# Keys before queries for B's first pair, and the residual's x loaded one slice per job

## The chip, the cores and the metric

The kernel runs on one core of a Trainium2 chip. The metric is the device time of one execution in microseconds (us). Times of engines and queues come from one profiled execution, counted from the start of its span.

## The reference

A decoder trunk of two layers over 1024 positions with 1024 channels. The change lies in layer 0, which reads (cut to what matters):

```
proj = (rmsnorm(x, g) * (1 + scale) + shift) @ w_in
a_q, a_k, a_v, b_q, b_k, b_v, f_logit, gate = split(proj)
a = swa_sink_attention(a_q, a_k, a_v, sinks, rel_bias)      # 8 heads, window 128, 2 key heads
b = forgetting_attention(b_q, b_k, b_v, log_sigmoid(f_logit + b_f))   # 8 heads, causal
x = x + gate_c * ((concat(a, b) * silu(gate)) @ w_out)      # the residual takes x once more
```

Layer 1 is a gated linear recurrence with a projection in, a convolution, a scan and a projection out; it is not touched.

## The kernel before, in words

All activations are kept with channels on the 128 partitions and positions along the free dimension, in two halves of 512 positions. A product of full precision is made of three matmuls: each operand is split into a high part (`hi`, a rounded copy made by ACT) and a low part (`lo`, the rest, made by POOL or DVE), and hi·hi, lo·hi and hi·lo are added up in PSUM.

**Attention.** The heads are worked in pairs: four pairs of A, then four of B. A pair is a row of units, each cut into steps: scores (S), a transpose of the probabilities on TensorE (T, `turn`), the product with the values (V, `product`) and, for A, an end step (E, `end`) that spreads the inverse sums with four transposes (`rbT_A`) and scales the output. A transposed block lies in one of the two PSUM buffers of the pool `psT` (`ps_t`); it is split by `split_t` (line 758) into `pth` (ACT) and `ptl` (DVE), and only then is its buffer free for the next transposes. The slots of lines 1052 to 1084 fix at which point each step comes.

**The fill.** Between these steps `weave` puts matmuls of projections that are needed later, so that TensorE always has something to do. `fill` (line 965) walks through a list of jobs. A job is a tile of weights, the k tiles, the activations and a `use` that takes the sums out of PSUM (tile `ps_fill`, two buffers); the weights of the next job are asked for when the job before it starts (line 980). While pair 3 of A is worked, the fill makes the queries and keys of B's first pair (`b_jobs(0)`, line 1018): `use_q` takes a half of the queries out of PSUM with two copies on ACT and two subtractions on DVE; `use_k` takes a half of the keys out with three copies on ACT, two subtractions and a copy on DVE, and two copies on POOL. The order of the two jobs is the list that `b_jobs` returns.

**The first out projection.** While the last pair of B is worked, the fill makes the first half of the out projection for seven of its eight k tiles: eight jobs, `o0_job(e)`, one for each tile of 128 output channels. At the end of each, `use_o0(e)` adds the sums to x on DVE (`residual`). That x is loaded again into the tile `x1_0`, whose memory is that of `hh_1` (the high part of the activations of the second half), which the fill of the pair before reads to its end. The eight loads, one per e, stand in a row at lines 1210 and 1211, just ahead of that `weave`.

**What sets the order.** TensorE's instructions stay in the order of the program (`ordered` holds "pe"). ACT, DVE, POOL and SP (the queue that issues nearly all DMAs) are put in order when the kernel is built, by a planner with an estimate of all durations: an instruction goes as soon as the planner has its inputs ready and its buffer free, the earlier one in the program first. `paced(name)` (line 87) pins instructions: each one issued inside it stays behind the instruction that the program has just before it on the same engine. On the chip each engine then takes its instructions strictly in that order, and one that waits holds up all behind it.

**Names.** `bq`, `khb`, `klb`: queries and high and low keys of B. `whi_o0a`, `wlo_o0a`: high and low weights of the eight jobs, split from `raw_o0a` as loaded. `pB`: a row of B's decay bias, loaded from DRAM (`gd`) on SP, masked at its end by POOL (`AFFINE_SELECT`), to which DVE adds the scores. Nearly all compute instructions are issued by one helper, so the profile gives L86 for them, and they are told apart by their tiles.

Of the kernel before, what the change touches and what calls it, by code (L numbers as in the profile page):

```python
# [27 lines left out]
KT = D // P  # L28
# [20 lines left out]
def hybrid_trunk(  # L49
# [43 lines left out]
    @contextmanager  # L93
    def paced(name):

        ordered.add(name)
        yield
        ordered.discard(name)

    act, dve, gp = Queue("act", nc.scalar), Queue("dve", nc.vector), Queue("gp", nc.gpsimd)  # L100
    pe, sync = Queue("pe", nc.tensor), Queue("sync", nc.sync)
# [38 lines left out]
    def hl_tile(slot, name, dt=F32R):  # L140
        return hl.tile([P, KT, HALF], dt, tag=f"hl{slot}", name=name)
# [56 lines left out]
    def t4(tag, name, dt=F32, bufs=None):  # L198
        bufs = bufs or BUFS[tag]
        return at.tile([P, 1024], dt, tag=tag, name=name, bufs=bufs)  # L200
# [97 lines left out]
    def split(raw, hi, lo, eng=gp):  # L298

        copy(hi, raw)  # L300
        sub(eng, lo, raw, r32(hi))
# [6 lines left out]
    def split_w(src, shape, name):  # L308
        return split_raw(load_w(src, shape, name), shape, name)
# [7 lines left out]
    def load_tile(src, name):  # L317
        parts = [split_w(src[:, 4 * i : 4 * i + 4], [P, 4, P], f"{name}_{i}") for i in range(2)]
        return [(parts[k // 4][0][:, k % 4], parts[k // 4][1][:, k % 4]) for k in range(KT)]
# [297 lines left out]
    def vtile(name):  # L617
        return at.tile([P, NB, 2, P], F32R, tag="V", name=name, bufs=2)

    va, vb0 = vtile("va"), vtile("vb0")  # L620
# [84 lines left out]
    def use_k(kh, kl):  # L705
        def use(h, ps):
            o = slice(h * HALF, (h + 1) * HALF)
            for hd, (a, b) in enumerate(((0, 64), (64, 0))):
                copy(kh[hd][a : a + 64, o], ps[a : a + 64])
                lo = kl[hd][a : a + 64, o]  # L710
                sub(dve, lo, ps[a : a + 64], r32(kh[hd][a : a + 64, o]))
                if hd:
                    dve.tensor_copy(kh[hd][b : b + 64, o], r32(kh[hd][a : a + 64, o]))
                else:
                    copy(kh[hd][b : b + 64, o], ps[a : a + 64])
                gp.tensor_copy(kl[hd][b : b + 64, o], r32(lo))

        return use
# [223 lines left out]
    def use_v(v, name):  # L942
        def use(h, ps):
            t = at.tile([P, HALF], F32, tag="tv", name=f"vt_{name}_{h}", bufs=1)
            copy(t, ps)

            def later():
                pt = ps_t(f"vT_{name}_{h}")
                for i in range(4):
                    tp(pt[:, i * P : (i + 1) * P], t[:, i * P : (i + 1) * P])  # L950
                for hd in range(2):
                    src = pt.rearrange("p (t h d) -> p t h d", t=4, h=2)[:, :, hd]
                    o = v[:, 4 * h : 4 * h + 4, hd]
                    copy(o[:, :, 0:64], src)
                    sub(dve, o[:, :, 64:128], src, r32(o[:, :, 0:64]))

            return later

        return use
# [36 lines left out]
    def lazy(make):  # L996

        got = []

        def get():  # L1000
            if not got:
                got.append(make())
            return got[0]

        return get

    def job(ti, name, use):
        return (lazy(lambda: load_tile(wt[ti], name)), range(KT), both, use)
# [4 lines left out]
    def q_job(ti, name):  # L1013
        q = lazy(lambda: qtiles(name))
        return q, job(ti, name, lambda h, ps: use_q(q(), name)(h, ps))

    def b_jobs(p):
        q, jq = q_job(T_BQ + p, f"bq_{p}")
        kh = lazy(lambda: [t4("KH", f"khb_{p}_{i}", F32R) for i in range(2)])
        kl = lazy(lambda: [t4("KL", f"klb_{p}_{i}", F32R) for i in range(2)])  # L1020
        jk = job(T_BK + p, f"bk_{p}", lambda h, ps: use_k(kh(), kl())(h, ps))
        if p == 0:
            return (lambda: (q(), kh(), kl(), vb0)), [jq, jk]
        v = lazy(lambda: vtile(f"vb{p}"))
        jv = job(T_BV + p - 1, f"bv_{p}", lambda h, ps: use_v(v(), f"bv_{p}")(h, ps))
        return (lambda: (q(), kh(), kl(), v())), [jq, jv, jk]
# [3 lines left out]
    for p in range(4):  # L1030
        q, jq = q_job(T_AQ + p, f"aq_{p}")
# [4 lines left out]
    for p in range(4):  # L1036
        src, js = b_jobs(p)
        jobs.append(js)
        starts.append(len(units))
        out = lazy(lambda p=p: heads_out(f"B_{p}"))  # L1040
        units += [unit_b(p, hd, j, src, out) for hd in range(2) for j in range(4)]
# [91 lines left out]
    def split_act(ti, h):  # L1133

        if h == len(yh):
            yh.append(hl_tile(3 * h, f"yh_{h}"))
            if h:
                tags = ("Q", "Q", "KH", "KL")
                yl.append(Parts([t4(t, f"yl_1_{i}", F32R) for i, t in enumerate(tags)]))
            else:  # L1140
                yl.append(hl_tile(1, "yl_0"))
        copy(yh[h][:, ti], gy[h][:, ti])
        sub(dve if ti % 2 and h else gp, yl[h][:, ti], gy[h][:, ti], r32(yh[h][:, ti]))
# [16 lines left out]
    def residual(xn, ps, lay, e):  # L1160
        dve.scalar_tensor_tensor(
            out=xn, in0=ps, scalar=mod[:, lay, 16 + e : 17 + e], in1=xn, op0=ALU.mult, op1=ALU.add
        )

    x1, w7, wo = [], [], []

    def use_o0(e):
        def use(h, ps):
            residual(x1[0][:, e], ps, 0, e)
            with paced("act"):  # L1170
                if e:
                    split_act(e - 1, 1)
            if e == 4:
                w7.append(at.tile([P, 2, KT, P], F32R, tag="V", name="w7"))
                for i in range(2):
                    es = slice(4 * i, 4 * i + 4)
                    raw = at.tile([P, 4, P], F32, tag="tv", name=f"w7raw_{i}", bufs=1)
                    sync.dma_start(raw, wo0.rearrange("e p k c -> p e k c")[:, es, KT - 1])
                    split(raw, w7[0][:, 0, es], w7[0][:, 1, es])

        return use

    def o0_job(e):
        def weights():
            with paced("act"):
                return load_tile(wo0[e], f"o0a_{e}")

        return (lazy(weights), range(KT - 1), lambda: {0: (yh[0], yl[0])}, use_o0(e))

    o0 = [o0_job(e) for e in range(KT)]  # L1190
    jobs.append(o0)
    jobs[7] = then_split(*jobs[7])
# [14 lines left out]


    x1.append(hl_tile(2, "x1_0", F32))
    for e in range(KT):  # L1210
        sync.dma_start(x1[0][:, e], xT[:, 0, e])
    split_act(KT - 2, 0)

    def load_o0c(e):
# [425 lines left out]
    for t0, tw in ((0, 512), (512, 256)):  # L1640
# [15 lines left out]
        for e in range(KT):  # L1656
            if t0 == 0 and e + 4 < KT:
                split_out(e + 4)
            w = wout[e]
# [161 lines left out]
```

## Time and profile before

| | |
|---|---|
| median of 3 runs | 871.53 us (871.23 to 871.74) |
| the profiled execution | 871.52 us, of it the span 869.7 us |
| mean granted TensorE clock | 0.996 |
| busy in the span: PE, DVE, ACT, POOL | 854.6, 573.7, 538.2, 374.6 us |
| DMA, mean over the span | 121 GB/s |

A row of a timeline gives start, duration, engine, operation, the tiles written and read, how many instructions were merged into the row, and in brackets how long the engine sat idle before it and what it waited for. `SPq` is the queue that issues DMAs; the time of its row is the issue, not the transfer. A row of the windows gives, for a stretch of time, the busy time of PE, PEld (weight loads), DVE, ACT and POOL with the number of instructions, the granted clock, the share of the DMA engines that were busy and the GB/s. In the list of waits stand the waiting tile, what ended the wait, the total in us, the count and the longest.

### The profile page before, as it was taken

Reading aid. Unit: us, or ns where it says so; the run is one execution under the profiler, and the core shown is the slowest. Engines: PE = TensorE matmul, PEld = TensorE weight load, DVE = VectorE, ACT = ScalarE, POOL = GpSimd, SP = SyncE. Lnnn points to the kernel's source line nnn. Section 1 sums busy time; section 2 is a strip of 40 time slices with the busy share of each in tenths; the row PEclk is TensorE's granted clock in tenths of the full one; section 3 lists DMA queues with packets and bytes.
Section 4 is the critical chain, followed back from the end, with each engine's and each line's share of the span. In section 5 each row is a group of like instructions: output and inputs, shape, how many; then the busy total and the mean of one; then the engine's idle time right before and its main releaser. Section 6 shows DMA issues by size and latency. Waiting matters only on the chain.

```text
span 869.7 us, 13308 instructions
## 1 busy us (share of the span) xinstructions
PE 854.6 (98%) x4553; PEld 724.7 (83%) x4553; DVE 573.7 (66%) x1131; ACT 538.2 (62%) x1052; POOL 374.6 (43%) x408
## 2 busy tenths in 40 slices
PE   9999999999999999999999999999999999999996
PEld 8788798888878888888888888878888877887996
DVE  7886567688777466566665678466676556973654
ACT  5766224688776565566766666457677666964731
POOL 4843232333342231232474554623655666875020
PEclk9999999999999999999999999999999999999999
DMA  9943772100113223223364464421212122226322
GB/s 342 403 180 128 222 238 76 43 25 25 37 44 115 89 80 125 93 90 119 100 209 143 158 206 170 134 78 61 80 55 73 44 66 80 96 86 205 111 109 86
DMA packets 54812, 104.88 MB, mean 121 GB/s; under 512 B 6888, under 2 KB 19632, under 8 KB 54232
## 3 DMA queue, kind: packets, MB, share of 16 engines
q1 hardware_dynamic: 53592, 102.98, 35.9%
q10 hardware_dynamic: 1152, 1.05, 0.4%
q8 instruction: 36, 0.59, 0.3%
q14 instruction: 32, 0.26, 0.1%
HBM read 95.07 MB, written 8.93 MB: 120 GB/s over the span
## 4 chain that ended last, share of the span: by engine, by line
PE 75%; DVE 6%; POOL 5%; DMA 5%; issue 4%; ACT 4%; SPq 0%; POOLq 0%; DVEq 0%; ACTq 0%
PE ps_fill L86 23%; PE ps_lx L86 6%; PE pst L86 6%; PE ps_o L86 5%; PE ps_o0c L86 5%; PE ps_lg L86 5%; PE oB L86 4%; PE ptB L86 3%; PE sB L86 3%; PE ps_t L86 3%; PE ps_v L86 3%; DMA ada<-in_ada_dram 2%; PE sA L86 2%; PE oA L86 2%; PE ptA L86 1%
## 5 line engine op out<-in xcount | busy, mean ns | idle before, releaser
L86 DVE TENSOR_TENSOR ptl_B<-ptB,pth_B 128x512 fp32r<-128x512 f32 (+1 forms) x80 | 50.9, 636 | 44.8 <-ACT pth_B L86 44.3
L86 ACT ACTIVATE pB<-pB,mnB 128x128 f32<-128x128 f32 (+3 forms) x64 | 49.5, 774 | 30.8 <-DVE mnB L86 30.5
L86 ACT ACTIVATE pth_B<-ptB 128x512 fp32r<-128x512 f32 (+1 forms) x80 | 44.1, 551 | 33.9 <-PE ptB L86 33.6
L86 DVE SCALAR_TENSOR_TENSOR xc_r<-ps_lx,col,xc_r 128x509 f32<-128x509 f32 (+2 forms) x48 | 35.6, 744 | 43.4 <-ACT xt_r L86 42.3
L86 POOL TENSOR_SCALAR_AFFINE_SELECT pB<-pB 128x128 f32<-128x128 f32 x64 | 19.0, 298 | 97.6 <-DMA pB<-gd 90.5
L86 PE MATMUL ps_o<-y1h,wo 128*128 128x512 f32 (+1 forms) x224 | 56.9, 342 | 0.7 <-POOL wo L86 0.7
L86 PE MATMUL pst<-hh,ws 128*128 128x512 f32 x192 | 55.4, 397 | 0.1
L86 PE MATMUL ps_lg<-h1h,wlo_lg 128*128 128x512 f32 x128 | 50.2, 392 | 0.9 <-POOL wlo_lg L86 0.7
L86 PE MATMUL ps_lx<-h1h,wlo_lx 128*128 128x512 f32 x128 | 50.4, 394 | 0.1
L86 PE MATMUL ps_lx<-h1l,whi_lx 128*128 128x512 f32 x128 | 50.3, 393 | 0.2 <-POOL h1l L86 0.2
L86 PE MATMUL ps_lx<-h1h,whi_lx 128*128 128x512 f32 x128 | 50.3, 393 | 0.0
L86 PE MATMUL ps_lg<-h1h,whi_lg 128*128 128x512 f32 x128 | 49.9, 389 | 0.0
L86 PE MATMUL ps_lg<-h1l,whi_lg 128*128 128x512 f32 x128 | 49.8, 389 | 0.0
L86 POOL TENSOR_TENSOR wlo_lx<-raw_lx,whi_lx 128x512 fp32r<-128x512 f32 x16 | 30.6, 1930 | 43.3 <-ACT whi_lx L86 34.0
L86 ACT ACT_TABLE_LOAD x35 | 44.9, 1283 | 5.1 <-issue 3.0
L86 PE MATMUL ptB<-ident,pB 128*128 128x128 f32 x288 | 45.0, 273 | 1.2 <-ACT pB L86 0.8
L86 PEld LDWEIGHTS ptB<-ident,pB 128*128 128x128 f32 x288 | 35.8, 140 | 11.7 <-ACT pB L86 1.7
L86 DVE CUSTOM_DVE_ANT_0 pB<-sB,pB 128x384 f32<-128x384 f32 (+2 forms) x64 | 35.2, 554 | 13.5 <-PE sB L86 7.7
L86 PEld LDWEIGHTS pst<-hh,ws 128*128 128x128 f32 x192 | 35.8, 188 | 9.3 <-issue 0.6
L86 PEld LDWEIGHTS ps_o<-y1h,wo 128*128 128x128 f32 x224 | 39.0, 189 | 5.5 <-POOL wo L86 1.1
L86 ACT ACTIVATE pA<-pA,mnA 128x256 f32<-128x256 f32 (+1 forms) x64 | 31.2, 488 | 11.5 <-DVE mnA L86 11.2
L86 PE MATMUL ps_o<-y1l,wo 128*128 128x512 f32 (+1 forms) x112 | 38.1, 340 | 0.0
(340 smaller groups left out, 2866.0 us busy)
## 6 DMA issues: line engine op xcount, KB each, us to landing
ada<-in_ada_dram SPq DMA_DIRECT2D x32, 512.0 KB
x<-in_xT_dram SPq DMA_DIRECT2D x20, 256.0 KB
ada<-in_ada_dram SPq DMA_DIRECT2D x4, 1024.0 KB
pB<-gd SPq DMA_DIRECT2D x8, 512.0 KB
raw_o0a<-in_wo_dram SPq DMA_DIRECT2D x16, 256.0 KB
raw_o0c<-in_wo_dram SPq DMA_DIRECT2D x16, 256.0 KB
x1d<-x SPq DMA_DIRECT2D x16, 256.0 KB
raw_lx<-in_wl_dram SPq DMA_DIRECT2D x16, 256.0 KB
```

Of the source, the lines that this page charges most:

```text
L86: ins = issue(*args, **kw)
```

## The change

Two edits. In `b_jobs` the two jobs of B's first pair trade places: keys first, then queries. And x for the residual of the first out projection is loaded in other places: slices 0 and 1 where all eight stood, and slice e + 1 right behind the loads of the weights of job e, for e from 1 to 6. (The weights of job 0 are asked for before `x1` holds a tile, so nothing is loaded with them.) The loads of the weights and of these slices are now also pinned on SP.

```diff
         if p == 0:
-            return (lambda: (q(), kh(), kl(), vb0)), [jq, jk]
+            return (lambda: (q(), kh(), kl(), vb0)), [jk, jq]
...
     def o0_job(e):
         def weights():
-            with paced("act"):
-                return load_tile(wo0[e], f"o0a_{e}")
+            with paced("act"), paced("sync"):
+                w = load_tile(wo0[e], f"o0a_{e}")
+                if e + 1 < KT and x1:
+                    load_x1(e + 1)
+                return w
...
+    def load_x1(e):
+        sync.dma_start(x1[0][:, e], xT[:, 0, e])
...
     x1.append(hl_tile(2, "x1_0", F32))
-    for e in range(KT):
-        sync.dma_start(x1[0][:, e], xT[:, 0, e])
+    for e in range(2):
+        load_x1(e)
     split_act(KT - 2, 0)
```

## The prediction

> **What bounds the kernel now.** I read the page first, then TensorE's waits, then the busy time by stretches of 10 us, and last the timelines around the two places that the change touches.
>
> ```profile
> span 869.7 us, 13308 instructions
> PE 854.6 (98%) x4553; PEld 724.7 (83%) x4553; DVE 573.7 (66%) x1131; ACT 538.2 (62%) x1052; POOL 374.6 (43%) x408
> ```
>
> TensorE is busy for 854.6 of 869.7 us. The change takes no matmul away and adds none, so all that it can give back is part of the 15.1 us in which TensorE stands. The list of its waits, largest first, shows what lies near the change.
>
> ```profile
> PE rbT_A L86 <- DVE ptl_A L86: 1.7, 1, 1.7
> ...
> PE oB L86 <- ACT pth_B L86: 0.5, 1, 0.5
> PE oB L86 <- DVE ptl_B L86: 0.4, 2, 0.2
> ```
>
> The longest single wait of TensorE in the whole kernel, 1.7 us, is that of the inverse sums of A (`rbT_A`) for DVE's `ptl_A`. The products of B (`oB`) wait for little. The stretches say where:
>
> ```profile
> 220.00:230.00 10.00, 10.00 (x60) 8.59 (x59) 7.74 (x20) 7.14 (x20) 0.79 (x4) 1.00 0.09 28
> 230.00:240.00 10.00, 10.00 (x63) 8.69 (x60) 6.33 (x19) 6.94 (x21) 5.28 (x9) 1.00 0.16 53
> ...
> 250.00:260.00 10.00, 8.23 (x58) 7.16 (x57) 8.69 (x26) 8.96 (x27) 4.48 (x11) 1.00 0.29 93
> ...
> 440.00:450.00 10.00, 9.57 (x64) 8.11 (x61) 5.76 (x15) 6.81 (x15) 8.06 (x10) 1.00 0.91 302
> 450.00:460.00 10.00, 10.00 (x59) 8.54 (x58) 6.27 (x16) 6.31 (x16) 5.10 (x7) 1.00 0.60 183
> 460.00:470.00 10.00, 9.63 (x51) 7.48 (x51) 5.27 (x14) 5.98 (x12) 5.55 (x6) 1.00 0.58 173
> ```
>
> In 250 to 260 TensorE is idle for 1.77 us, with ACT at 8.96 and DVE at 8.69 of 10: here A's last units meet the second half of B's keys, and ACT and DVE are the bound. In 440 to 450, where the eight loads of x stand, the DMA engines are at 0.91, but TensorE idles for 0.43 us only, then for 0.00 and 0.37. So the most that edit one can give is about 1.7 us and edit two about 0.8 us.
>
> **Edit one, keys ahead of queries.** The place in detail, TensorE, then ACT, then DVE:
>
> ```profile
> 253.41 0.60 PE L86 MATMUL ptA<-ident,pA 128*128 128x128 f32 x4
> ...
> 258.48 0.63 PE L86 MATMUL rbT_A<-ident,rb_A 128*128 128x128 f32 x4 [1.69 <-DVE ptl_A L86]
> ```
>
> ```profile
> 254.06 1.19 ACT L86 ACTIVATE khb<-ps_fill 64x512 fp32r<-64x512 f32 x2
> ...
> 256.80 0.60 ACT L86 ACTIVATE pth_A<-ptA 128x512 fp32r<-128x512 f32 x1
> ```
>
> ```profile
> 255.80 0.69 DVE L86 TENSOR_TENSOR klb<-ps_fill,khb 64x512 fp32r<-64x512 f32 x1
> 256.52 0.42 DVE L86 CAST khb<-khb 64x512 fp32r<-64x512 f32 x1
> ...
> 257.44 0.29 DVE L86 CUSTOM_DVE_ANT_0 pB<-sB,pB 128x128 f32<-128x128 f32 x1
> ...
> 257.65 0.69 DVE L86 TENSOR_TENSOR ptl_A<-ptA,pth_A 128x512 fp32r<-128x512 f32 x1
> ```
>
> `rbT_A` needs one of two transpose buffers. The one that comes free next holds the transposes of 253.41, done at 254.01; ACT takes them up only at 256.80, since it works through the key copies (254.06, two in a row, 1.19 us) and what has piled up behind. DVE has 0.69 and 0.42 us of the keys in its way too, and its `ptl_A` ends at 258.34. `rbT_A` starts 0.14 us later.
>
> What a half of queries and a half of keys cost:
>
> ```profile
> L86 ACT ACTIVATE bq<-ps_fill x4: 574/592/593, 225.9 to 236.8; 64x512 fp32r<-64x512 f32 x4
> L86 DVE SCALAR_TENSOR_TENSOR bq<-ps_fill,bq x4: 683/688/693, 226.5 to 237.4; 64x512 fp32r<-64x512 f32 x4
> ```
>
> ```profile
> L86 ACT ACTIVATE khb<-ps_fill x6: 576/592/596, 242.7 to 254.7; 64x512 fp32r<-64x512 f32 x6
> L86 DVE TENSOR_TENSOR klb<-ps_fill,khb x4: 676/689/695, 243.3 to 255.8; 64x512 fp32r<-64x512 f32 x4
> L86 DVE CAST khb<-khb x2: 422/422/423, 246.3 to 256.5; 64x512 fp32r<-64x512 f32 x2
> ```
>
> ```profile
> L86 POOL CAST klb<-klb x4: 605/698/866, 244.2 to 256.6; 64x512 fp32r<-64x512 f32 x4
> ```
>
> These views cover both halves. One half of queries: ACT 2 x 0.592 = 1.18 us, DVE 2 x 0.688 = 1.38 us, POOL nothing. One half of keys: ACT 3 x 0.592 = 1.78, DVE 2 x 0.689 + 0.422 = 1.80, POOL 2 x 0.698 = 1.40 us. With the order turned, the last half before B begins costs 0.59 us less on ACT and 0.42 us less on DVE. One of the two copies at 254.06 goes, so `pth_A` starts at about 256.21 and ends at 256.81; on DVE the copy at 256.52 goes, and `ptl_A` ends at 258.34 - 0.42 = 257.92 in the order of now, or at 256.81 + 0.69 = 257.50 if it is put ahead of the row of `pB`. The wait of 1.69 falls to between 1.27 and 0.85 us. I take 0.5 us of gain, near the order as it is. The bounds are 0 (the planner orders ACT or DVE another way and the time is not passed on) and the whole wait, 1.69. What is late next is the same chain for the following transposes: ACT stays nearly full up to 260.
>
> What moves the other way: keys now come out of PSUM at about 226 and 235 us, which puts 0.59 us on ACT, 0.42 on DVE and 1.40 on POOL twice. I cost it at nothing: TensorE shows 10.00 of 10 there, ACT has 2.9 and 3.1 us free in those stretches, DVE 2.3 and 3.7, POOL 9.2 and 4.7. With that cover gone it would be at most 2 x 0.59 = 1.2 us. The two pairs of weight loads that trade places are of one size, and DMA shares of 0.09 and 0.16 hide them. No wait is added: the first scores of B need the first half of both, and the later of the two comes out at about 243 us in either order.
>
> **Edit two, the loads of x.** SP's issues around the row, then POOL's steps on what was loaded, with an undisturbed load from another place for comparison:
>
> ```profile
> 435.64 2.38 SPq L86 DMA_DIRECT2D raw_o0a<-in_wo_dram  x2
> 439.82 3.65 SPq L86 DMA_DIRECT2D x<-in_xT_dram  x8
> 443.58 1.13 SPq L86 DMA_DIRECT2D pB<-gd  x2
> ```
>
>
> ```profile
> 449.25 0.29 POOL L86 TENSOR_SCALAR_AFFINE_SELECT pB<-pB 128x128 f32<-128x128 f32 x1 [1.77 <-DMA pB<-gd]
> ```
>
> ```profile
> 251.96 0.33 SPq L86 DMA_DIRECT2D pB<-gd  x1
> ```
>
> ```profile
> 254.90 0.29 POOL L86 TENSOR_SCALAR_AFFINE_SELECT pB<-pB 128x128 f32<-128x128 f32 x1 [0.49 <-DMA pB<-gd]
> ```
>
> The eight issues take 3.65 us, 0.46 each. Behind them, at 443.58, comes the bias for the next scores, and POOL gets it at 449.25, 5.67 us after its issue; the undisturbed load of 251.96 was there after 2.94 us. With six of the eight issues gone from the row, that bias is issued up to 6 x 0.46 = 2.7 us earlier and lands up to 2.7 us sooner after it. But TensorE's own waits here, 0.43 and 0.37 us, are not for this bias: the scores lie in PSUM meanwhile, and the fill goes on. So I take 0.2 us of the 0.8 us, with bounds of 0 and 0.8.
>
> The other side is that the loads of `raw_o0a` are now pinned. Six slices of x still have to go, each 0.46 us on SP, spread over the jobs. Their use is far off:
>
> ```profile
> L86 DVE SCALAR_TENSOR_TENSOR x<-ps_fill,mod,x x8: 743/748/751, 452.2 to 514.7; 128x512 f32<-128x512 f32 x8
> ```
>
> Eight residuals from 452.2 to 514.7 make (514.7 - 452.2) / 7 = 8.93 us for a job. Slice e + 1 is issued with the weights of job e, at the start of job e - 1, and used at the end of job e + 1: three jobs, 26.8 us, against a landing within 2.94 to 5.67 us. So these loads cost nothing; if SP held them by more than 21 us, the residual would wait. The Trainium skill speaks against this edit: "DMA: Bandwidth & Descriptors", Rules for kernel authors, says that a DMA should be issued early and waited for late, and the edit issues six loads later. By that rule the time would rise; it has its place among the rivals.
>
> The pin matters for the weights of job 1. In the kernel before, the two loads at 435.64 went ahead of the row of x (they are the second half of tile 1 and the first of tile 2, counted over the sixteen). Now both loads of tile 1 stand behind slice 1 in the program, and the slices wait for the memory of `hh_1`, to 439.82. So they are issued at 439.82 + 2 x 0.46 = 440.74 and at 441.20.
>
> ```profile
> L86 ACT ACTIVATE whi_o0a<-raw_o0a x16: 615/622/632, 432.0 to 498.9; 128x512 fp32r<-128x512 f32 x16
> ```
>
> ```profile
> 441.71 1.15 ACT L86 ACTIVATE whi_o0a<-raw_o0a 128x512 fp32r<-128x512 f32 x2
> 442.76 0.48 ACT L86 ACTIVATE pth_B<-ptB 128x384 fp32r<-128x384 f32 x1
> ```
>
> ACT's copies of tile 1 are the second pair of the sixteen, at 441.71. With a landing after 2.94 to 5.67 us the data are there at 443.7 to 446.9. Job 1 starts when job 0 ends, about 452.2, and needs 2 x 0.62 us on ACT and POOL's part between, so the weights themselves come in time. What is queued behind a copy that waits is all of ACT, first of all `pth_B`, for which TensorE's products wait. I expect the planner to move the copies behind the ACT work that is ready, which costs 0; the bounds are 0 and 5.2 us (446.9 - 441.71).
>
> **The sum.** The profiled execution took 871.52 us, 1.8 us more than its span, and the median of the runs, 871.53, is the same. 871.5 - 0.5 (keys) - 0.2 (row of x) = 870.8 us. A measurement of this kernel can tell about 0.2% from no change, 1.74 us; the forecast lies inside.
>
> **The rivals.**
>
> Rival one, the whole wait goes: the planner, with less in ACT's and DVE's way, puts `pth_A` and `ptl_A` ahead, and the waits of 440 to 470 shrink by half. For it speaks that the needed transposes were done at 254.01, so 4.3 us passed before they were out, of which only 1.3 us are work on them. Against it: ACT is at 8.96 of 10 and loses only 0.59. Time: 871.5 - 1.7 - 0.4 = 869.4 us.
>
> Rival two, slower: ACT waits at the copy of tile 1's weights. It decides if the planner's estimate of the landing is shorter than the chip's, so that the copy stays ahead of `pth_B`. For it speaks that POOL waited 1.77 us for a bias in the same crowd; against it that fewer loads now crowd there. ACT would stand from 441.71 to between 443.7 and 446.9, so 2.0 to 5.2 us; part of it falls into ACT's free time, and I take 2.5 us for TensorE: 871.5 - 0.5 + 2.5 = 873.5 us.
>
> Rival three, the load on ACT is only moved: the keys at 226 and 235 make a wait as large as the one that shrinks. Against it stands TensorE's 10.00 in both stretches. Time: 871.5 us.
>
> Rival four, by the rule above, the slices come late: a residual waits and keeps its PSUM buffer, so the fill stands. It needs a delay of over 21 us on SP. If it came, each of six jobs could lose up to a landing of 2.94 us; with one such loss 871.5 - 0.5 + 2.9 = 873.9 us.
>
> **How the numbers follow.** Forecast 0.46, rival one 0.30, rival two 0.13, rival three 0.08, rival four 0.03. Faster by over 0.2% (below 869.8) is rival one: 0.30. Slower by over 0.2% (above 873.3) is rivals two and four: 0.16. The rest, forecast and rival three, is 0.54. The range goes from 869.2, just below rival one, to 872.8, where the smallest of rival two's waits ends (871.5 - 0.5 - 0.2 + 2.0); left out are the lower part of rival one and the upper of rivals two and four, together about 0.2.
>
> **What would show it.** In the changed profile the keys leave PSUM near 226 and 235 us and the queries near 243 and 251; between 250 and 260 ACT falls by about 0.6 and DVE by about 0.4 us per the same work, and the wait of `rbT_A` stands at 0.8 to 1.3 us. SP shows two slices of x at about 440 and six single ones after it, and POOL's step on the next bias comes 3 to 5 us sooner than 449.25. Wrong would be a wait of `rbT_A` unchanged or gone, a new wait of TensorE at 220 to 240, or ACT's copies of `whi_o0a` waiting for a DMA with `pth_B` behind them and `oB` late at 444 to 448.

## The result, and the profile after

The changed kernel takes 874.94 us (median of 10 runs, 873.59 to 876.77) against 871.46 us for the kernel before in the same comparison. The ratio is 1.0033, with a 95% interval of 1.0024 to 1.0042: slower by about 3 us, on the other side of no change than the forecast of 870.8, and above the range's end of 872.8. Timed a second time on another chip (below) it gave 1.0029 (1.0018 to 1.0040). The profiled execution of after took 873.92 us with a span of 872.1; before it was 871.52 and 869.7. So the two traces, laid side by side, have to account for 2.40 us. That is near the difference of the medians on the second chip (874.36 - 871.92 = 2.44), and 1.1 us less than the one on the first, where the profiled execution of after was its second fastest of ten. Two executions far out of line, one of 2359.56 us in the second timing of the change and one of 1717.87 us with `w7raw` apart in the kernel before, are counted in the medians and left out of the ratios.

The list of TensorE's waits of the changed kernel, largest first and cut to two lines (total, count, longest in us):

```profile
PE ptB L86 <- ACT pB L86: 3.2, 3, 2.4
...
PE rbT_A L86 <- DVE ptl_A L86: 0.9, 1, 0.9
```

One wait has shrunk, `rbT_A` from 1.7 to 0.9 us. Another stands at the head of the list now: the transposes of B's probabilities wait for ACT 3.2 us in all, where it was 0.8 in the kernel before, and 2.4 us of that is a single new wait. The stretches of the changed kernel that answer to those of before:

```profile
220.00:230.00 10.00, 10.00 (x60) 8.59 (x59) 7.16 (x20) 7.60 (x21) 1.98 (x6) 1.00 0.08 28
230.00:240.00 10.00, 10.00 (x62) 8.69 (x61) 6.95 (x21) 7.52 (x22) 6.33 (x12) 1.00 0.15 53
250.00:260.00 10.00, 8.93 (x64) 7.86 (x63) 8.61 (x25) 8.78 (x27) 2.96 (x9) 1.00 0.33 91
440.00:450.00 10.00, 7.60 (x40) 6.36 (x39) 3.97 (x12) 6.17 (x14) 7.02 (x9) 0.83 0.63 204
```

Between 250 and 260 TensorE is idle for 1.07 us in place of 1.77 and does 64 matmuls in place of 58; at 220 to 240, where the keys now leave PSUM, it is still at 10.00. That is edit one, and it works. Between 440 and 450 TensorE does 40 matmuls where before it did 64, and the granted clock is 0.83, which is 3.4 us at half clock.

Where the time went can be read off by counting matmuls: their order on TensorE is fixed but for the two jobs that trade places, so the start of the n-th one can be compared between two traces. Difference to the kernel before, in us, from the starts in each trace:

| n-th matmul (start in before) | 1400 (253.05) | 1500 (271.04) | 2480 (441.03) | 2500 (444.78) | 2550 (453.17) | 2700 (480.21) | last (862.48) |
|---|---|---|---|---|---|---|---|
| after | -0.05 | -0.80 | -0.86 | +1.43 | +2.20 | +2.34 | +2.35 |

The keys win 0.8 us near 255 us, and this is kept for 170 us. Then 2.29 us are lost within 20 matmuls, 0.77 more within the next fifty, and 0.15 after that: -0.81 + 2.29 + 0.77 + 0.15 = 2.40 us from the 1400th matmul on, or 2.35 with the 0.05 that after was ahead there. After the 2700th nothing more is lost.

The place of the loss in the changed kernel. First SP's issues:

```profile
438.96 0.81 SPq L86 DMA_DIRECT2D x<-in_xT_dram  x2
439.82 0.90 SPq L86 DMA_DIRECT2D raw_o0a<-in_wo_dram  x2
440.76 0.43 SPq L86 DMA_DIRECT2D x<-in_xT_dram  x1
441.30 0.84 SPq L86 DMA_DIRECT2D pB<-gd  x2
```

Next ACT, with the time that it stood idle in brackets:

```profile
440.84 0.49 ACT L86 ACTIVATE pth_B<-ptB 128x384 fp32r<-128x384 f32 x1
444.12 0.63 ACT L86 ACTIVATE whi_o0a<-raw_o0a 128x512 fp32r<-128x512 f32 x1 [2.79 <-DMA raw_o0a<-in_wo_dram]
444.66 1.13 ACT L86 ACTIVATE pB<-pB,mnB 128x1024 f32<-128x1024 f32 x1
...
445.79 0.61 ACT L86 ACTIVATE whi_o0a<-raw_o0a 128x512 fp32r<-128x512 f32 x1
```

And TensorE:

```profile
443.26 0.27 PE L86 MATMUL ptB<-ident,pB 128*128 128x128 f32 x1
445.93 0.55 PE L86 MATMUL ptB<-ident,pB 128*128 128x128 f32 x3 [2.40 <-ACT pB L86]
```

Read backwards: TensorE's three transposes wait for the exponentials of a row of 1024 of `pB`. ACT makes these at 444.66, right after its copy of tile 1's weights, and that copy had stood at the head of ACT's queue since 441.33 for a load that SP issued at 439.82. In the kernel before, the same row of 1024 was made at 443.13, with no wait ahead of it:

```profile
443.13 1.15 ACT L86 ACTIVATE pB<-pB,mnB 128x1024 f32<-128x1024 f32 x1
```

A copy whose result was wanted about ten microseconds later (job 0's last step, the residual, is at 454.41) held up work that TensorE needed at once.

### The profile page after: what moved, and what is told of

It is laid out like the page before. It is cut to its first block, busy times and chain, and to the rows that moved or that the text cites. A ratio compares the mean times of both kernels' runs of the same rounds, so it can differ in the third digit from the quotient of the medians.

```text
span 872.1 us, 13306 instructions
## 1 busy us (share of the span) xinstructions
PE 855.7 (98%) x4553; PEld 725.7 (83%) x4553; DVE 573.5 (66%) x1131; ACT 538.2 (62%) x1052; POOL 374.1 (43%) x408
## 3 DMA queue, kind: packets, MB, share of 16 engines
q10 hardware_dynamic: 1152, 1.05, 0.4%
## 4 chain that ended last, share of the span: by engine, by line
PE 76%; DVE 6%; DMA 6%; POOL 4%; ACT 4%; issue 3%; SPq 1%; POOLq 0%; DVEq 0%; ACTq 0%
PE ps_fill L86 23%; PE ps_lx L86 6%; PE ps_lg L86 6%; PE pst L86 6%; PE ps_o L86 5%; PE ps_o0c L86 5%; PE oB L86 4%; PE sB L86 3%; PE ptB L86 3%; PE ps_v L86 3%; PE ps_t L86 3%; DMA ada<-in_ada_dram 2%; PE sA L86 2%; PE oA L86 1%; PE ptA L86 1%
```

## The experiments

The theory: the loss comes from the pin of the weights' loads on SP, which puts tile 1's loads behind the slices of x; ACT then stands at its copy. The rivals: keys first costs something later; the slices of x as such cost; the fall of the granted clock after the wait is a loss of its own. The kernels of each table row ran on one chip with the kernel before between them.

| run | median, us | before, us | ratio (95%) |
|---|---|---|---|
| keys first alone | 871.24 | 872.20 | 0.9987 (0.9978 to 0.9996) |
| x per job with pins alone | 875.17 | 872.20 | 1.0036 (1.0024 to 1.0049) |
| pin of the weights alone | 874.64 | 872.20 | 1.0032 (1.0019 to 1.0044) |
| change, weights not pinned | 871.82 | 872.20 | 1.0000 (0.9992 to 1.0009) |
| change, weights ahead of x | 871.16 | 871.56 | 0.9996 (0.9988 to 1.0005) |
| change, TensorE busy in the wait | 874.05 | 871.56 | 1.0027 (1.0016 to 1.0037) |
| weights not pinned, w7raw apart | 869.95 | 871.56 | 0.9982 (0.9973 to 0.9991) |
| the change again | 874.36 | 871.92 | 1.0029 (1.0018 to 1.0040) |
| TensorE busy in the wait, again | 874.10 | 871.92 | 1.0023 (1.0012 to 1.0033) |
| before, w7raw apart | 871.31 | 871.92 | 0.9997 (0.9988 to 1.0006) |
| keys first, w7raw apart | 871.08 | 871.92 | 0.9988 (0.9980 to 0.9997) |

The profiled executions of these runs, by the same count of matmuls against the kernel before:

| n-th matmul | 1400 | 1500 | 2480 | 2500 | 2550 | 2700 | last |
|---|---|---|---|---|---|---|---|
| keys first alone | +1.05 | +0.29 | +0.26 | +0.25 | +2.58 | +2.38 | +2.49 |
| x per job with pins alone | +0.51 | +0.52 | +0.52 | +2.85 | +3.00 | +3.68 | +3.62 |
| pin of the weights alone | +0.81 | +2.32 | +2.32 | +1.99 | +4.24 | +4.23 | +4.17 |
| weights not pinned | -0.01 | -0.82 | -0.87 | -0.87 | -1.08 | -0.17 | -0.22 |
| weights ahead of x | +0.03 | -0.72 | -0.79 | -0.79 | -1.06 | -0.40 | -0.46 |
| not pinned, w7raw apart | +0.08 | -0.71 | -0.73 | -0.73 | -1.00 | -2.30 | -1.65 |
| the change again | +0.33 | -0.42 | -0.42 | +1.50 | +2.60 | +2.86 | +2.83 |
| before, w7raw apart | +0.13 | +0.07 | -0.03 | -0.04 | +0.20 | -1.11 | -0.95 |
| keys first, w7raw apart | +0.66 | -0.10 | -0.03 | -0.04 | +0.70 | -0.57 | -0.34 |

What a row has at the 1400th matmul is from ahead of both edits; only what it gains or loses from there on counts.

**Keys first alone.**

```diff
-            return (lambda: (q(), kh(), kl(), vb0)), [jq, jk]
+            return (lambda: (q(), kh(), kl(), vb0)), [jk, jq]
```

> The kernel before with the keys ahead of the queries and nothing else. Theory (the loss is all in the loads, the keys gain): the wait of the inverse sums of A falls from 1.69 to about 0.95 us as in the changed kernel, no wait of 2.4 us at 443, granted clock 1.00 in 440 to 450; time 0.7 us under the kernel before, about 870.8. Rival (the keys spoil the plan of ACT later on): slower than the kernel before by over 1 us.

Faster, 871.24 against 872.20 us, and its wait of `rbT_A` is 0.9 us. Edit one is a small gain by itself. The execution that was profiled was this kernel's slowest (874.08) and shows something else. POOL stood for the next bias, and ACT then for DVE's row maximum over it. POOL, then ACT:

```profile
451.53 0.54 POOL L86 TENSOR_SCALAR_AFFINE_SELECT pB<-pB 128x128 f32<-128x128 f32 x2 [4.30 <-DMA pB<-gd]
```

```profile
452.19 0.40 ACT L86 ACTIVATE pB<-pB,mnB 128x128 f32<-128x128 f32 x1 [4.06 <-DVE mnB L86]
```

That bias was issued at 443.84, behind the row of eight slices, and POOL got it 7.7 us later, where it was 5.67 us in the kernel before. In this execution 2.33 us are lost between the 2500th and the 2550th matmul; TensorE waits 1.32 us there for `pth_B`, and the granted clock is at half from 454.6 to 458.0. So the row of eight does cost something, in some executions; it is the thing that edit two was to take away.

**x per job with its pins alone, queries first as before.**

```diff
-            with paced("act"):
-                return load_tile(wo0[e], f"o0a_{e}")
+            with paced("act"), paced("sync"):
+                w = load_tile(wo0[e], f"o0a_{e}")
+                if e + 1 < KT and x1:
+                    load_x1(e + 1)
+                return w
...
-    for e in range(KT):
+    for e in range(2):
```

> The loads of x one slice per job and pinned with the weights, queries ahead of keys as before. Theory: the long wait of the transposes near 444 us (2.4 us in the changed kernel) and the dip of the granted clock stay, the wait of the inverse sums stays at 1.69; time about 0.7 us over the changed kernel and 4 us over the kernel before, about 875.5. Rival (the keys made it): no such wait, 871.5.

The whole loss is here. ACT of this run, then TensorE:

```profile
445.54 0.63 ACT L86 ACTIVATE whi_o0a<-raw_o0a 128x512 fp32r<-128x512 f32 x1 [2.83 <-DMA raw_o0a<-in_wo_dram]
```

```profile
447.36 0.55 PE L86 MATMUL ptB<-ident,pB 128*128 128x128 f32 x3 [2.45 <-ACT pB L86]
```

The waits are those of after, 2.79 and 2.40 us there, although the queries come first: keys first has no part in the loss.

**The pin of the weights alone; x stays in one row of eight.**

```diff
-            with paced("act"):
+            with paced("act"), paced("sync"):
                 return load_tile(wo0[e], f"o0a_{e}")
```

> The kernel before with its eight slices in one row, queries first, and only the loads of the eight weight tiles pinned on SP. Theory (the pin makes it): the loads of tile 1 stand behind all eight slices, are issued near 443.5 and land near 449; ACT stands at the copy or, with the copy planned later, the weights come closer to their use at 452; a wait of TensorE of 1 to 4 us, time 872.5 to 876. Rival (the spreading of the slices makes it): as the kernel before, 871.5.

No slice of x is moved here, and the time, 874.64 us, is near that of the run above, with overlapping intervals. SP, then ACT:

```profile
442.15 3.65 SPq L86 DMA_DIRECT2D x<-in_xT_dram  x8
445.85 0.98 SPq L86 DMA_DIRECT2D raw_o0a<-in_wo_dram  x2
```

```profile
452.25 0.63 ACT L86 ACTIVATE whi_o0a<-raw_o0a 128x512 fp32r<-128x512 f32 x1 [3.04 <-DMA raw_o0a<-in_wo_dram]
```

With the pin, tile 1's loads stand behind all eight slices, and ACT waits 3.04 us. The copy stands elsewhere in ACT's order than in the change, behind the row of 1024, and TensorE's longest wait here is one of 1.02 us for `pth_B`. The execution that was profiled is this kernel's slowest (875.67). Of what it is behind, 1.5 us were lost between the 1400th and the 1500th matmul, where the clock was at half and which lies long before tile 1's loads; 1.9 us were lost from the 2480th on. So one word of code, in a line that the change gives no weight to, is enough for a loss of about that size, by a wait of the same kind.

**The change with the slices pinned and the weights not.**

```diff
-            with paced("act"), paced("sync"):
+            with paced("act"):
                 w = load_tile(wo0[e], f"o0a_{e}")
+            with paced("sync"):
                 if e + 1 < KT and x1:
                     load_x1(e + 1)
-                return w
+            return w
```

> The changed kernel with the pin on SP taken from the weights and left on the slices of x, so keys first and one slice per job, but the weights of tile 1 free to be loaded ahead of the slices. Theory: tile 1 is loaded near 401 and 435 us as in the kernel before, ACT doesn't stand at its copy, no clock dip; time about 870.7. Rival (one slice per job costs by itself): 873 to 875 as the changed kernel.

The wait of 2.4 us is gone, and the time is 871.82 us, where I had expected about 870.7. By the matmuls, the keys' gain is kept to the 2500th (-0.87) and 0.21 us more is won by the 2550th. But it ends level with the kernel before. ACT, then TensorE:

```profile
461.42 0.63 ACT L86 ACTIVATE w<-w7raw 128x512 fp32r<-128x512 f32 x1 [3.58 <-DMA w7raw<-in_wo_dram]
462.07 0.60 ACT L86 ACTIVATE pth_B<-ptB 128x512 fp32r<-128x512 f32 x1
```

```profile
462.72 0.51 PE L86 MATMUL oB<-pth_B,vb 128*128 128x256 f32 x2 [0.72 <-ACT pth_B L86]
```

It is the same pattern at a second place: a copy of weights (the eighth k tile, `w7raw`, whose second load has to wait until the first is split, since they share a buffer) stands ahead of `pth_B` on ACT. The copy can start at about the same time as in the kernel before, so whoever comes earlier only waits longer:

```profile
461.63 0.63 ACT L86 ACTIVATE w<-w7raw 128x512 fp32r<-128x512 f32 x1 [2.69 <-DMA w7raw<-in_wo_dram]
```

One comparison on this chip is against the slices: keys first with x in one row took 871.24 us, 0.58 less than this run. The loss at `w7raw` may be the reason, but keys first alone was profiled only in its slowest execution, so it isn't shown that it does not lose as much there.

**The change with tile 1's weights asked for ahead of the slices.**

```diff
+    o0[1][0]()
     x1.append(hl_tile(2, "x1_0", F32))
-    for e in range(2):
+    for e in range(3):
         load_x1(e)
```

> The change with everything pinned as it is, but the two loads of tile 1's weights issued ahead of the two x slices of the row, so ahead of the wait for the memory of hh_1 that held them to 439.82 us. If the loss comes from the copies of tile 1's weights standing on ACT for a late load (2.79 us of wait at 444.12, 2.40 us of TensorE's), SP should show those loads before 437 us, ACT's copies should stand without a wait near 442, TensorE's wait of ptB for pB should be under 0.3 us, and the time should be that of the change less 2.3 to 3.1 us: 870.8 to 871.8 us. If pinning on SP as such costs (the queue held in the order of the program), or the later issue of the x slices does, the time stays over 873 us although the wait of ptB is gone.

SP of this run (the first row has some idle time of the queue between its two issues, the second is at 434.63):

```profile
429.90 5.06 SPq L86 DMA_DIRECT2D raw_o0a<-in_wo_dram  x2
439.03 1.29 SPq L86 DMA_DIRECT2D x<-in_xT_dram  x3
```

```profile
440.40 1.15 ACT L86 ACTIVATE whi_o0a<-raw_o0a 128x512 fp32r<-128x512 f32 x2
```

Everything is pinned here as in the change, the slices go one per job after the first three, as there, and the loss is gone: 871.16 us. So neither the pin nor the slices cost the 2 to 3 us as such. What costs is the place of two loads: in the change they are issued at 439.82, 1.5 us before ACT is ready for them (441.33), and here by 434.63, 5.8 us ahead of the copy.

**TensorE kept busy in the wait.** The single transpose at 443.26 is made 25 times over, on the same data.

```diff
-                    tp(pt[:, w : w + P], prs[r][:, m * P : (m + 1) * P])
+                    for _ in range(25 if (hx, j, m, r) == (5, 3, 0, 0) else 1):
+                        tp(pt[:, w : w + P], prs[r][:, m * P : (m + 1) * P])
```

> The change with the one 128x128 transpose that stood alone before TensorE's wait of 2.40 us (ptB at 443.26) done 25 times over instead of once, so TensorE is at work in what was a wait; it rewrites the same block, the result is the same, and ACT waits for its load as before. In the change the granted clock fell to half for 3.4 us right after that wait. If the half clock follows from TensorE's idling, it should not be seen near 446 to 450 us in this run, the clock's mean should be higher by about 0.004, and the time should be 0.7 to 1.5 us under the change's: 873.4 to 874.2 us, still over the kernel before. If the half clock comes from something else, or the wait of ACT alone is the whole loss, the time stays within 0.4 us of the change's 874.9.

> The changed kernel once more, unaltered, on the same chip as the next run, because the two were so far timed on different chips and their ratios to the kernel before (1.0033 and 1.0027) lie within each other's intervals. Expected as before: 874 to 876 us. If the profiled execution shows no interval of half clock after the wait of 2.4 us, that interval is not a fixed consequence of the wait.

> The run with the transpose repeated 25 times in the wait, unaltered, beside the change on one chip. Its profiled execution had no half clock near 446 us and a wait of ACT of 3.04 us, and ended as late as the change's. If the half clock is a regular part of the change's loss, this stays 0.5 to 1.0 us under the change on the same chip. If it is only there in some executions and ACT's wait is the loss, the two agree within 0.4 us.

The first run with the wait filled took 874.05 us, inside the 873.4 to 874.2 that I had written for a half clock that costs. But it ran on another chip than the change, and its ratio of 1.0027 lies inside the change's interval; so the two were timed again side by side.

The reason for this pair of kernels is a row of the stretches of after, right behind the wait (the clock is the last number but two):

```profile
446.50:449.50 3.00, 3.00 (x13) 2.57 (x13) 2.41 (x7) 2.05 (x6) 2.37 (x4) 0.50 0.13 37
```

TensorE's clock was granted at half for some 3 us. The change again, on another chip: its wait, and the stretch behind it:

```profile
446.00 0.55 PE L86 MATMUL ptB<-ident,pB 128*128 128x128 f32 x3 [2.03 <-ACT pB L86]
```

```profile
446.50:449.50 3.00, 2.67 (x14) 2.09 (x13) 2.34 (x7) 2.00 (x6) 1.43 (x4) 0.60 0.39 113
```

And the second run with the wait filled, TensorE and the same stretch:

```profile
443.32 3.22 PE L86 MATMUL ptB<-ident,pB 128*128 128x128 f32 x28
```

```profile
446.50:449.50 3.00, 2.31 (x16) 1.85 (x15) 2.15 (x7) 2.14 (x7) 2.39 (x4) 1.00 0.71 217
```

This fits a half clock that comes from TensorE's standing: 0.50 and 0.60 with the wait, 1.00 in both filled runs, while ACT waited as long in them (2.73 us in this one). Two executions of each are few, as the next case shows. But on one chip the two kernels take 874.36 and 874.10 us, 0.26 apart, inside the 0.4 that I had put down for "ACT's wait is the loss". The profiled pair tells why: the filled kernel gains 0.63 us on the change by the 2520th matmul, and by the 2650th all but 0.15 of it is given back, since the steps behind wait for ACT and DVE. The waits of the filled kernel's TensorE between 440 and 470 us:

```profile
PE ptB L86 <- DVE ptl_B L86: 0.7, 1, 0.7
PE oB L86 <- ACT pth_B L86: 0.6, 1, 0.6
```

In the change on the same chip these two are 0.3 us and none. The run of x per job with pins says the same of the loss. It had a wait of 2.45 us and no half clock behind it:

```profile
447.50:450.50 3.00, 2.27 (x16) 1.84 (x16) 2.00 (x7) 1.99 (x6) 2.78 (x6) 1.00 0.25 75
```

and it still lost 3.62 - 0.52 = 3.1 us behind the 2480th matmul, as after did (2.35 + 0.86 = 3.2). So the half clock is there in the records, but as a term of the loss it can't be told from nothing here.

**w7raw's two loads in two jobs.** First in the kernel with unpinned weights, then in the kernel before, then with keys first and x in one row:

```diff
-            if e == 4:
+            if e == 3:
                 w7.append(at.tile([P, 2, KT, P], F32R, tag="V", name="w7"))
-                for i in range(2):
+            if e in (3, 4):
+                i = e - 3
...
-                    split(raw, w7[0][:, 0, es], w7[0][:, 1, es])
+                with paced("act"):
+                    split(raw, w7[0][:, 0, es], w7[0][:, 1, es])
```

> The run with the pin on the x slices alone (no pin on the weights' loads), and besides it the two loads and splits of the eighth k tile's weights (w7raw, one buffer for both) asked for in two jobs, e = 3 and e = 4, in place of both in e = 4. There ACT waited 3.58 us at 461.42 for the second w7raw load (2.69 in the kernel before), and about 0.9 us of the keys' gain was lost in the same stretch. If that wait gave the gain away, it should be under 1 us here, and the time 870.5 to 871.1 us, under the kernel before by about 0.9 us. If the gain is lost to something else (ACT's copies themselves, or the x slices' place), the time stays within 0.3 us of that run's 871.8.

> The kernel before, and only w7raw's two loads and splits in jobs e = 3 and e = 4 with the copies pinned on ACT, in place of both in e = 4. No edit of the change in it. ACT's wait of 2.69 us for the second load should go. If the gain of that edit stands by itself, 870.3 to 871.2 us against about 871.6; if it only gives back what the x slices' move had cost, within 0.3 us of the kernel before.

> Keys ahead of queries, the eight x slices in one row as before, and w7raw's two loads and splits in two jobs. Against the run that has both of these and x one slice per job (869.95 us, ratio 0.9982) it tells what the x slices' move itself is worth with no load of weights held up by it: if the row of eight costs by holding the next bias, this is 0.3 to 0.8 us slower than that run (870.3 to 870.8); if the move is worth nothing, the same (869.7 to 870.2).

ACT's copies in the first of the three:

```profile
478.94 0.62 ACT L86 ACTIVATE w<-w7raw 128x512 fp32r<-128x512 f32 x1
488.57 0.63 ACT L86 ACTIVATE w<-w7raw 128x512 fp32r<-128x512 f32 x1 [0.67 <-DMA w7raw<-in_wo_dram]
```

The wait of 3.58 us is 0.67 now. Between the 2550th and the 2700th matmul, where the kernel without this edit lost 0.91 us (-1.08 to -0.17), this one wins 1.30 more (-1.00 to -2.30), and it keeps half of that to the end. The time is 869.95 us, the fastest version of this study at 0.9982 of the kernel before (0.9973 to 0.9991), whose interval leaves out both no change and the kernel after. I had expected 870.5 to 871.1 us, about 0.9 under the kernel before; it is 1.6 us under (871.56 - 869.95). In the kernel before the same edit took 0.6 us off the median, but its interval of 0.9988 to 1.0006 holds no change. ACT's wait for the second load is gone there, and the time lies between my two cases. With keys first and the row of eight the ratio is 0.9988, and 871.08 us is outside both ranges that I had given. The profiled execution of that one loses 0.74 us between the 2500th and 2550th matmul, where the one with x per job gains 0.27. ACT of the two, in that order:

```profile
450.81 0.40 ACT L86 ACTIVATE pB<-pB,mnB 128x128 f32<-128x128 f32 x1 [2.97 <-DVE mnB L86]
```

```profile
447.19 0.40 ACT L86 ACTIVATE pB<-pB,mnB 128x128 f32<-128x128 f32 x1
448.25 0.51 ACT L86 ACTIVATE pB<-pB,mnB 128x256 f32<-128x256 f32 x1 [0.56 <-DVE mnB L86]
```

The same step on a row of 128 stands 2.97 us behind the row of eight and not at all behind three slices. By the trace that is worth 1.0 us. By the times 0.9982 and 0.9988 on two chips, whose intervals overlap, it isn't shown.

## Why the prediction was wrong

**What bounds the kernel: right.** TensorE's waits were all there was to win or lose; the 2.40 us between the two profiled executions are found in them and in what follows on them.

**Edit one: right in mechanism, low in size.** I took 0.5 us with a remaining wait of 0.85 to 1.27. It is 0.95:

```profile
256.15 0.60 ACT L86 ACTIVATE pth_A<-ptA 128x512 fp32r<-128x512 f32 x1
...
256.86 0.69 DVE L86 TENSOR_TENSOR ptl_A<-ptA,pth_A 128x512 fp32r<-128x512 f32 x1
...
257.69 0.63 PE L86 MATMUL rbT_A<-ident,rb_A 128*128 128x128 f32 x4 [0.95 <-DVE ptl_A L86]
```

`pth_A` starts at 256.15 (256.21 was worked out) and `ptl_A` ends at 257.55 (257.50, for the case that DVE puts it ahead of the row of `pB`). Of the two cases that I gave, the better one came; TensorE gained 0.75 us by the 1500th matmul. The cover for the keys at 225 to 240 held, with TensorE at 10.00.

**Edit two, the row of x: right on the bias, not shown as a gain.** POOL's step on the next bias came at 446.05 in place of 449.25, 3.2 us sooner, within the 3 to 5 that I named (0.9 of it is the lead that the keys had won):

```profile
446.05 0.29 POOL L86 TENSOR_SCALAR_AFFINE_SELECT pB<-pB 128x128 f32<-128x128 f32 x1
```

In the change that is not seen in the time, because the new wait lies on top of it. Without that wait the 0.2 us that I took is there in the traces: 0.21, 0.27 and 0.27 us are won between the 2500th and 2550th matmul in the three runs that keep the slices apart and do not hold up the weights. Three runs with the row of eight and no pin lose 0.24, 0.74 and 2.33 us there, all against the one execution of the kernel before, which has the row too. In the times it isn't shown: on one chip the row of eight was 0.58 us the faster (871.24 against 871.82), and with `w7raw` apart the slices were ahead, but on two chips and with overlapping intervals. The six slices later on cost nothing, as said: the eight residuals of after, at 454.4 to 517.1, waited for TensorE's sums or for nothing, never for x:

```profile
462.56 0.75 DVE L86 SCALAR_TENSOR_TENSOR x<-ps_fill,mod,x 128x512 f32<-128x512 f32 x1 [1.60 <-PE ps_fill L86]
...
509.36 0.75 DVE L86 SCALAR_TENSOR_TENSOR x<-ps_fill,mod,x 128x512 f32<-128x512 f32 x1 [0.22 <-PE ps_fill L86]
```

So rival four did not come true for x. What was issued late, at a cost, were the loads beside x, the weights.

**The pin of the weights: the step that failed.** Its first half stood. Both loads behind the slices, at 440.74 and 441.20: they went at 439.82 and 440.34. Landing at 443.7 to 446.9: ACT's copy began at 444.12. Then came "I expect the planner to move the copies behind the ACT work that is ready, which costs 0; the bounds are 0 and 5.2 us". It moved one of the two, to 445.79. The other stayed where it was, and the term was 2.29 us on TensorE, plus 0.77 and 0.15 behind it, in which lie the half clock and the steps that followed late; their shares aren't shown. Up to this place the keys alone had won 0.8 us, as much as both terms of gain in the sum (0.7), so this term put the time on the other side of no change.

It was not the only term that was missing. With the pin off the weights the ratio was 1.0000 (0.9992 to 1.0009), with the forecast's 0.9992 at the very end of the interval. The trace has 0.91 us lost between the 2550th and the 2700th matmul, where ACT waits for `w7raw`. The sum had no term for that place.

Rival two was this case. Its place and price were nearly those measured (873.5 us; 2.5 us on TensorE), and it got 0.13. It had one detail wrong: `pth_B` was not behind the copy but ahead of it, at 440.84; what stood behind was the exponentials. Was there a reason in what I had before me for another weight? One: the code pins the copies on ACT as well, so a copy can move back only as far as the program's order and the planner's own estimate of the load let it, and my step gave it a freedom that nothing in the trace of before showed. There the two copies at 441.71 had no wait at all and so told nothing about what the planner does with late data. That the planner thought the data would be there by 441 is my reading of the order; no run shows its estimate.

The range ended at 872.8, below rival two's full price; with that rival at 0.13 and rival four above it, the upper end cut off the case at its full price, which is what came.

## What to carry to other kernels

A load is in time if it lands before its consumer comes up in its engine's order; that can be long before the result is needed. When a change puts loads in a new order on the issuing queue, look for the consumer's place in its engine's order, and ask what stands behind it. A pin that is added along with an edit is an edit of its own and wants a price of its own; here it cost more than the two edits gave. And where a gain melts away later, look for a second place of the same kind: the late `w7raw` took back 0.7 to 0.9 us in two runs, and nothing in the one with its loads put apart.

## What the runs showed of the hardware

A wait of TensorE of some 2 us can be followed by half clock: behind 2.40 and 2.03 us in the change, and in the run with the pin alone behind the same wait of 1.7 us for `ptl_A` that the kernel before has:

```profile
261.00:264.00 3.00, 3.00 (x13) 2.73 (x12) 1.84 (x7) 1.10 (x4) 1.98 (x3) 0.50 0.00 0
```

In the slowest execution of keys first alone it stood behind a wait of 1.32 us. It does not always follow: not behind 2.45 us in the run of x per job with pins, nor behind the 1.69 us in the profiled execution of the kernel before. That may be part of why single executions of one kernel lie 2 to 3 us apart (870.8 to 873.87 for the kernel before); it wasn't tested. The Trainium skill, "TensorE: Matmul & The Clock Gate", Why this matters for your kernels, asks that no gap exceed about 3 us. Here waits of 1.3 to 2.4 us stood ahead of half clock in some executions, so what was measured is stricter. The Trainium skill, the same page, Part 1, says that the window in which activity is judged runs freely and does not reset when a kernel starts. That would fit a wait that is followed by half clock in one execution and not in the next, but no run here sets the phase of that window.
